# The two halves of the split weights in one buffer, column beside column, in a two-layer hybrid block

## The chip, the cores and the metric

The kernel runs on one core of one Trainium2 chip. The metric is device time in microseconds from launch to end, as the median of repeated runs. The engines are called PE (TensorE; PEld is its weight load), DVE (VectorE), ACT (ScalarE), POOL (GpSimd) and SP (the queue that issues most DMAs).

## The reference

Two layers over 512 tokens of width 1024, in float32. Each layer adds three things to x in turn. First a mixer: one wide projection of the normed x, then three branches (a retention, a gated delta rule with a triangular solve, a dilated attention), each projected back, gated, summed and projected once more. Then an attention to 256 memory tokens. Then a convolved, gated MLP of width 2816.

```python
for l in range(DEPTH):
    x = x + hybrid_mixer(rms_norm(x, norm_mix_g[l]), positions, w_in[l], ...)
    x = x + memory_cross_attention(rms_norm(x, norm_xattn_g[l]), rms_norm(mem, norm_mem_g[l]),
                                   xattn_wq[l], xattn_wkv[l], xattn_wo[l])
    x = x + conv_gated_mlp(rms_norm(x, norm_ffn_g[l]), ffn_w_up[l], ffn_conv_w[l], ffn_conv_b[l],
                           ffn_w_down[l])
return rms_norm(x, final_norm_g)
```

What matters here are the products of x (or of what comes from it) with a weight matrix. They make up nearly all of the arithmetic.

## The kernel before

All weights lie in device memory as slabs of 128 partitions and up to 1024 columns, in the order in which they are used. `slab_load` brings one slab by a DMA of the SP queue into `w`, of which there are two buffers. `slab` cuts it into pieces of `part` columns (512, but for one product) and splits each piece into two parts whose sum is the weight: ACT copies the piece into `wh` in the type fp32r, which rounds it (L203), and DVE subtracts `wh` from `w` and leaves the rest in `wl` (L204). `wh` and `wl` are tiles of their own, 528 columns or 2112 bytes in each partition, with three buffers each. Both instructions are put ahead of other work by `first()`.

The other operand is split in the same way (`xgh`, `xgl` and the like), and `mm3` forms a product of the two sums by three matmuls: high by high (L214), then L215, then L216. The fourth, low by low, is left out. Two kinds of product use it:

- Products with features on the partitions of the result (`fm_tile`, called by `fm_one` and `fm_group`). The weights are the stationary operand, 128 columns to a weight load, and the tokens stream by as the moving operand, 512 at a time (256 for the memory's keys `km`, and for the last tile of the last layer, which is done in two halves). L214 and L215 read `wh`, L216 reads `wl`. A piece of 512 columns has 4 k tiles or column tiles, so 12 matmuls.
- Products with tokens on the partitions (`tm_group`: `rva`, `rvb`, `rg`, `z`, `dv0`, `dv12`, `vm`). Here the tokens are the stationary operand and the weights stream. L214 and L216 read `wh`, L215 reads `wl`. `dv12` takes every 4th token as its stationary columns. `some = 528 // n` says how many k tiles a piece holds. For `rva`, n is 264: two k tiles make a piece of 528 columns, and a slab of three k tiles gives a piece of 528 and one of 264.

The program is laid out by a planner (the Tile framework): it takes the instructions with their priorities, gives each tile a buffer when one of its tag is released, fixes the order on each engine and sets the semaphore waits. A buffer is released when the last instruction that reads or writes its tile is done. Every engine works its own list in order.

The order of stages in a layer: norm sums, `rva` (half of the retention's values and the decays), the gated delta rule's keys, queries and values (`g`), its triangular solve on DVE (lines `fs`, `Tg`), its scan over four blocks, between them the retention's products and further projections (`rqk`, `rvb`, `rg`, `z`, `dqk`, `dv0`, `dv12`), the dilated attention (`ds`, `dt`, `do`), into which the gates (`gate`, `y`) are woven, `wo`, the memory attention (`km`, `xq`, `vm`, `xo`), and the MLP (`up`, `ua`, `uu`, `dn`, at the very end `dl`).

Of the kernel before, what the change touches and what calls it, by code (L numbers as in the profile page):

```python
# [10 lines left out]
F32R = mybir.dt.float32r  # L11
# [21 lines left out]
# The reference's inverse frequencies, which depend on no input.  # L33
# [16 lines left out]
# columns of the constants  # L50
# [6 lines left out]
# columns of the parameters  # L57
# [4 lines left out]
# column ranges of w_in  # L62
# [39 lines left out]
def tile_hybrid(ctx, tc, xT, memT, pos, wts, cst, kst, prm, rows, outT):  # L102
# [53 lines left out]
    def over(ap, n):  # L156
        """[p, a] as [p, a, n], each element n times."""
        a = ap.shape[1]
        return ap.rearrange("p (a o) -> p a o", o=1).to_broadcast([ap.shape[0], a, n])

    def again(ap, n):
        """[p, f] as [p, n, f], n times."""
        return ap.rearrange("p (o f) -> p o f", o=1).to_broadcast([ap.shape[0], n, ap.shape[1]])

# [26 lines left out]
    def slab(n, part=512):  # L191
        """The next slab; part(o, m) gives the two parts of its columns o to o + m."""
        pieces = []
        with first():
            if not loaded:
                slab_load()
            l, s, size, w = loaded.pop(0)
            assert size == n, (l, s, size, n)
            for o in range(0, n, part):
                m = min(part, n - o)  # L200
                wh = wp.tile([P, 528], F32R, tag="wh", name=f"wh{l}_{s}_{o}", bufs=3)
                wl = wp.tile([P, 528], F32R, tag="wl", name=f"wl{l}_{s}_{o}", bufs=3)
                S.activation(wh[:, :m], w[:, o:o + m], AF.Copy)  # L203
                V.tensor_tensor(wl[:, :m], w[:, o:o + m], wh[:, :m], ALU.subtract)  # L204
                pieces.append((wh, wl))

        def cols(o, m):
            h, lo = pieces[o // part]
            assert o % part + m <= part
            return h[:, o % part:o % part + m], lo[:, o % part:o % part + m]  # L210
        return cols
# [6 lines left out]
    def fm_tile(out, w, off, mv, kts, start=True, stop=True, tok=slice(None)):  # L218
        """out[cols, tokens] += W[kts, cols]^T mv[kts]; the weights of the kts stand from off on."""
        for i, kt in enumerate(kts):  # L220
            mm3(out, *w(off + i * P, P), mv[0][:, kt, tok], mv[1][:, kt, tok],
                start and i == 0, stop and i == len(kts) - 1)
# [6 lines left out]
    def fm_group(names, mv, nk):  # L229
        """Four output tiles, a pair of k tiles after the other."""  # L230
        outs = [pd(n) for n in names]
        for k0 in range(0, nk, 2):
            kts = list(range(k0, min(k0 + 2, nk)))
            w = slab(len(kts) * P * len(outs))
            for m, o in enumerate(outs):
                fm_tile(o, w, m * len(kts) * P, mv, kts, k0 == 0, kts[-1] == nk - 1)
        return outs

    def tm_group(name, st, n, kper, tok=blk, nt=NB, pools=(pd,) * NB):
        """out[tokens, cols] for each block of tokens."""  # L240
        outs = [pools[b](f"{name}{b}", (n,)) for b in range(nt)]
        for k0 in range(0, KT, kper):
            kts = list(range(k0, min(k0 + kper, KT)))
            some = 528 // n
            w = slab(len(kts) * n, some * n)
            for i0 in range(0, len(kts), some):
                for b in range(nt):
                    for i in range(i0, min(i0 + some, len(kts))):
                        kt = kts[i]
                        mm3(outs[b], st[0][:, kt, tok(b)], st[1][:, kt, tok(b)], *w(i * n, n),  # L250
                            kt == 0, kt == KT - 1)
        return outs

    def rsqrt(y, v):
        """y = v ** -0.5 by Newton's steps from an estimate by the bits."""
        n = v.shape[1]
        t = small("nt", 32, 2)[:, :n]
        yi = y.bitcast(I32)
        V.tensor_scalar(yi, v.bitcast(I32), 1, None, ALU.arith_shift_right)
        V.tensor_scalar(yi, yi, -1, 0x5F3759DF, ALU.mult, ALU.add)  # L260
        for _ in range(3):
            V.tensor_tensor(t, y, y, ALU.mult)
            V.scalar_tensor_tensor(t, t, -0.5, v, ALU.mult, ALU.mult)
            V.scalar_tensor_tensor(y, t, 1.5, y, ALU.add, ALU.mult)

# [1 line left out]
    def feed(xt, gcol, oh, ol):  # L267
        """x * g in two f32r parts."""
        S.activation(oh, xt, AF.Identity, scale=gcol)
        V.scalar_tensor_tensor(ol, xt, gcol, oh, ALU.mult, ALU.subtract)  # L270
# [9 lines left out]
    def rms(acc, nb, name, perm=False, row=None):  # L280
        """1 / rms as columns [token of the block, block] (then of the blocks of every 4th token) and as rows."""
        rc = small("rc", 8, 3)

        def column(o, tok):
            sp = pg(f"{name}_ss{o}", (nb,))
            for b in range(nb):
                PE.matmul(sp[:, b:b + 1], lhsT=acc[:, tok(b)], rhs=one, start=True, stop=True)
            v = small("rv", 4)[:, :nb]
            V.tensor_scalar(v, sp, 1.0 / D, EPS, ALU.mult, ALU.add)
            rsqrt(rc[:, o:o + nb], v)  # L290

        column(0, blk)
        rps = pg(name + "_rp", (nb * P,))
        for b in range(nb):
            PE.matmul(rps[:, blk(b)], lhsT=rc[:, b:b + 1].to_broadcast([P, P]), rhs=ident,
                      start=True, stop=True)
        rr = tmp("row", [T], name + "_row", 1) if row is None else row
        S.activation(rr, rps, AF.Copy)
        if perm:
            column(nb, lambda b: slice(b, None, NB))  # L300
        return rc, rr
# [52 lines left out]
    def load_tab(j, k0, k1, rr):  # L354
        """The two tables with 1 / rms in them, and the constants of a branch."""
# [7 lines left out]
    def gated(dst, p, rc, half, b, grow):  # L363
        """dst = (1 + tanh(z / 2)) * z / rms' * g, with z = p * rms', for one block of tokens."""
# [6 lines left out]
    def conv_gdn(dst, p, rr, w, name):  # L371
        """dst = 2 silu(conv(p * rr))."""
# [17 lines left out]
    def gdn_decays(l, ab, rb):  # L390
        """Decays and rates: minus the running log decays gp (by tokens of each block), their exponentials,
        and exp(-|gp_i - gp_j|) below the diagonal (in A) and from it on (in attn)."""
# [46 lines left out]
    def norms_of(pool, j, h, src, ssv):  # L439
        """Sums of squares of one head's vectors."""  # L440
# [6 lines left out]
    def gdn_inverse(l, kT, ssv, beta, eg, A):  # L447
        """U = ((I + A)^-1)^T, with A the decayed products of the keys below the diagonal, in A's place."""
# [14 lines left out]
        # diagonal blocks of 32 by substitution, one on each of 64 partitions  # L463
# [27 lines left out]
        # from 32 to 64  # L491
# [18 lines left out]
        # from 64 to 128  # L510
# [24 lines left out]
    def gdn_scan(l, kT, qT, vb, U, attn, ceg, eg, egl, ekl):  # L535
        """The states over the blocks; returns the raw outputs and their sums of squares."""
# [58 lines left out]
    def retention(l, rqk, rv, dec):  # L595
        """Scores within blocks of 128 tokens; what stands before a block comes as a state."""
# [44 lines left out]
    def head_out(o, ssq, gz, rc, scale, oh, ol, pst, name):  # L641
        """The heads' norms, the gates, and the outputs with features on the partitions, in two parts."""
# [24 lines left out]
    def dilated(l, dq, dk, dv0, dv12, kc):  # L667
        """Group 0 over blocks of 128 tokens, groups 1 and 2 over every 4th token; one softmax over all."""
# [5 lines left out]
        for i, o in enumerate((oA, oB)):  # L674
            v8 = st[i].rearrange("p (n e) -> p n e", e=8)
            for n in range(NB):
                for hh in range(2):
# [3 lines left out]
                    # heads hh and hh + 2 stand on the same rows of the array  # L681
# [41 lines left out]
        # the share of each set in the sum over both  # L723
# [37 lines left out]
    def branch(l, j, o, nk, per, rr, merged, last=None):  # L761
        """merged += (1 + tanh(gate / 2)) * (o @ w)."""
# [127 lines left out]
    def update(x, m, p, scale, then):  # L890
        """x += scale * p for one tile of features, and what is next for it."""
# [10 lines left out]
    def cross(l, mm, mrc, mrow, rr, oh, ol):  # L902
        """Attention to the memory: K with features, V with memory tokens on the partitions."""
# [3 lines left out]
        def parts(h, lo, p, row, name):  # L907
            """p * row in two parts."""
# [56 lines left out]
    def final(x, p, t, n):  # L965
        """What follows the last feature tile, for n tokens from t on."""
# [104 lines left out]
    for l in range(L):  # L1071
# [7 lines left out]
        # the memory's norm  # L1079
# [46 lines left out]
def feature_tiles(w, cols):  # L1126
    """[tile, 128, k tiles * 128]: for each tile of 128 columns, its k tiles side by side."""
# [4 lines left out]
def feature_group(w, cols, per=2):  # L1132
    """Slabs of `per` k tiles for all columns: [128, column tile, k tile, 128]."""
# [5 lines left out]
def token_group(w, cols, per):  # L1139
    """Slabs of `per` k tiles: [128, k tile, columns]."""  # L1140
# [9 lines left out]
def slabs_of(i, l):  # L1150
# [4 lines left out]
    # partners of a rotation 16 apart, within 32 partitions  # L1155
# [45 lines left out]
def columns(a):  # L1201
    """[..., k * 128] as [128, ... * k]."""
# [74 lines left out]
```

## Time and profile before

| what | value |
|---|---|
| time, median of 3 runs | 2179.11 us (2178.05 to 2179.14) |
| span of the profiled execution | 2177.5 us |
| PE busy | 2138.7 us, 10665 matmuls |
| PEld busy | 1776.8 us |
| DVE busy | 1369.2 us |
| ACT busy | 927.7 us |
| split of the weights, ACT L203 | 683 instructions, 429.0 us |
| split of the weights, DVE L204 | 683 instructions, 499.7 us |
| granted TensorE clock, mean | 0.991 of full speed |

The profile is one execution of the program. Busy time is the time in which an engine works on an instruction of the program. Matmuls are pipelined: the next starts before the one before it has ended, so the length of one matmul's row (about 0.39 us at 512 columns) is not its share of the time. The distance from one start to the next is. Idle time stands with the instruction before which the engine was idle, and with what released it.

### The profile page before, as it was taken

Reading aid. Unit: us, or ns where it says so; the run is one execution under the profiler, and the core shown is the slowest. Engines: PE = TensorE matmul, PEld = TensorE weight load, DVE = VectorE, ACT = ScalarE, POOL = GpSimd, SP = SyncE. Lnnn points to the kernel's source line nnn. Section 1 sums busy time; section 2 is a strip of 40 time slices with the busy share of each in tenths; the row PEclk is TensorE's granted clock in tenths of the full one; section 3 lists DMA queues with packets and bytes.
Section 4 is the critical chain, followed back from the end, with each engine's and each line's share of the span. In section 5 each row is a group of like instructions: output and inputs, shape, how many; then the busy total and the mean of one; then the engine's idle time right before and its main releaser. Section 6 shows DMA issues by size and latency. Waiting matters only on the chain.

```text
span 2177.5 us, 28783 instructions
## 1 busy us (share of the span) xinstructions
PE 2138.7 (98%) x10665; PEld 1776.8 (82%) x10665; DVE 1369.2 (63%) x2565; ACT 927.7 (43%) x1879; POOL 392.3 (18%) x403
## 2 busy tenths in 40 slices
PE   7899999999999999999999999999999999999997
PEld 7678888888888888888888888978888888888886
DVE  7994585435577775377488846643455787745654
ACT  5734234434355444244356242443344564433433
POOL 6721120001130211011122122100111211100112
PEclk9999999989999999999999999999999999999999
DMA  4324232222333232332323422322223323232332
GB/s 143 90 95 104 77 101 79 59 92 86 99 97 97 88 97 92 102 95 91 112 100 88 115 79 69 92 78 75 75 95 97 107 88 97 90 99 92 97 91 83
DMA packets 69756, 201.58 MB, mean 93 GB/s; under 512 B 18352, under 2 KB 21168, under 8 KB 69104
## 3 DMA queue, kind: packets, MB, share of 16 engines
q1 hardware_dynamic: 67120, 192.34, 28.7%
q0 software_dynamic: 2352, 7.37, 1.2%
q8 instruction: 83, 1.36, 0.3%
q14 instruction: 57, 0.47, 0.1%
q10 hardware_dynamic: 144, 0.04, 0.0%
HBM read 192.85 MB, written 6.88 MB: 92 GB/s over the span
## 4 chain that ended last, share of the span: by engine, by line
PE 87%; DVE 8%; DMA 1%; ACT 1%; issue 1%; SPq 0%; DVEq 0%; ACTq 0%
PE gate L214 4%; PE gate L215 4%; PE gate L216 4%; PE ua L216 3%; PE uu L216 3%; PE uu L214 3%; PE ua L214 3%; PE uu L215 3%; PE ua L215 3%; PE dn L216 3%; PE dn L215 3%; PE dn L214 3%; PE dqk L214 2%; PE dqk L216 2%; PE dqk L215 2%; DVE wl L204 2%
## 5 line engine op out<-in xcount | busy, mean ns | idle before, releaser
L203 ACT ACTIVATE wh<-w 128x512 fp32r<-128x512 f32 (+2 forms) x683 | 429.0, 629 | 868.6 <-PE dn L215 136.6
L204 DVE TENSOR_TENSOR wl<-w,wh 128x512 fp32r<-128x512 f32 (+2 forms) x683 | 499.7, 733 | 386.8 <-ACT wh L203 363.0
L214 PE MATMUL gate<-xgh,wh 128*128 128x512 f32 x384 | 157.6, 410 | 0.0
L215 PE MATMUL gate<-xgl,wh 128*128 128x512 f32 x384 | 156.1, 406 | 0.0
L216 PE MATMUL gate<-xgh,wl 128*128 128x512 f32 x384 | 156.0, 406 | 0.0
L216 PE MATMUL ua<-xgh,wl 128*128 128x512 f32 x320 | 126.2, 394 | 0.0
L216 PE MATMUL uu<-xgh,wl 128*128 128x512 f32 x320 | 126.2, 394 | 0.0
L214 PE MATMUL uu<-xgh,wh 128*128 128x512 f32 x320 | 126.0, 394 | 0.0
L214 PE MATMUL ua<-xgh,wh 128*128 128x512 f32 x320 | 126.0, 394 | 0.0
L215 PE MATMUL ua<-xgl,wh 128*128 128x512 f32 x320 | 125.8, 393 | 0.0
L215 PE MATMUL uu<-xgl,wh 128*128 128x512 f32 x320 | 125.7, 393 | 0.0
L214 PE MATMUL dn<-ah,wh 128*128 128x512 f32 x308 | 121.2, 394 | 0.0
L215 PE MATMUL dn<-al,wh 128*128 128x512 f32 x308 | 121.1, 393 | 0.0
L216 PE MATMUL dn<-ah,wl 128*128 128x512 f32 x308 | 117.7, 394 | 0.0
L1017 POOL TENSOR_TENSOR fya<-fya,fyu 128x512 f32<-128x512 f32 x44 | 72.9, 1657 | 228.7 <-DVE fyu L1001 223.3
L278 POOL TENSOR_TENSOR acc<-acc,sq 128x512 f32<-128x512 f32 x41 | 59.3, 1445 | 250.2 <-ACT sq L277 249.2
L778 POOL TENSOR_TENSOR mg<-mg,g 128x512 f32<-128x512 f32 x32 | 45.9, 1435 | 301.1 <-DVE g L776 301.1
L214 PEld LDWEIGHTS gate<-xgh,wh 128*128 128x128 f32 x384 | 75.0, 195 | 18.5 <-issue 2.6
L216 PEld LDWEIGHTS gate<-xgh,wl 128*128 128x128 f32 x384 | 74.6, 194 | 17.5 <-issue 0.7
L215 PEld LDWEIGHTS gate<-xgl,wh 128*128 128x128 f32 x384 | 74.9, 195 | 16.6 <-issue 0.4
L351 POOL TENSOR_TENSOR rot<-rot,tab 128x512 f32<-128x512 f32 x32 | 47.7, 1501 | 170.4 <-DVE rot L350 160.6
L216 PE MATMUL g<-xgh,wl 128*128 128x512 f32 x192 | 76.8, 400 | 1.6 <-DVE wl L204 1.6
(497 smaller groups left out, 5267.4 us busy)
## 6 DMA issues: line engine op xcount, KB each, us to landing
w<-in_wts SPq DMA_DIRECT2D x331, 512.0 KB, 3.5
tab<-tabs_d POOLq DMA_DIRECT2D x4, 512.0 KB, 4.2
mem<-in_memT POOLq DMA_DIRECT2D x8, 256.0 KB, 3.7
x<-in_xT SPq DMA_DIRECT2D x2, 1024.0 KB, 5.2
x_d<-x SPq DMA_DIRECT2D x8, 256.0 KB, 4.0
x<-x_d SPq DMA_DIRECT2D x2, 1024.0 KB, 5.6
out<-x SPq DMA_DIRECT2D x8, 256.0 KB, 2.3
w<-in_wts SPq DMA_DIRECT2D x7, 256.0 KB, 2.6
```

The costliest lines, as they stand in the source:

```text
L203: S.activation(wh[:, :m], w[:, o:o + m], AF.Copy)
L204: V.tensor_tensor(wl[:, :m], w[:, o:o + m], wh[:, :m], ALU.subtract)
L214: PE.matmul(out, lhsT=lh, rhs=rh, start=start, stop=False)
L215: PE.matmul(out, lhsT=lh, rhs=rl, start=False, stop=False)
L216: PE.matmul(out, lhsT=ll, rhs=rh, start=False, stop=stop)
L278: eng.tensor_tensor(acc, acc, sq, ALU.add)
L351: G.tensor_tensor(t, t, tab[:, 1, :], ALU.mult)
L778: G.tensor_tensor(mt, mt, g, ALU.add)
L1017: G.tensor_tensor(ya, ya, yu, ALU.mult)
```

## The change

The two tiles `wh` and `wl` become one tile `wt` of 1040 floats (4160 bytes) in each partition, of which 1024 are used, with three buffers. `slab` has a new argument `turns`. With `turns`, which all products with features on the partitions use, `wh` is every second float of `wt` from the first on and `wl` every second from the second on: the high and the low part of a column stand side by side, and the columns of either part are 8 bytes apart. Without it (`tm_group`), `wh` is the first half of the 1024 floats and `wl` the second half, each contiguous as before.

With 1024 floats a piece holds at most 512 columns, so `some` becomes `512 // n`. For `rva` that is 1 where it was 2: its pieces have 264 columns, and its slabs of 792, 792 and 528 columns give 3, 3 and 2 pieces. For n of 256 and 512 nothing changes. The instructions that split, load and multiply are the same otherwise, and so are the DMAs. All comments of the file were taken out or left as empty lines, which changes line numbers by a few and no instruction.

```diff
-    def slab(n, part=512):
+    def slab(n, part=512, turns=True):
...
             for o in range(0, n, part):
                 m = min(part, n - o)
-                wh = wp.tile([P, 528], F32R, tag="wh", name=f"wh{l}_{s}_{o}", bufs=3)
-                wl = wp.tile([P, 528], F32R, tag="wl", name=f"wl{l}_{s}_{o}", bufs=3)
+                wt = wp.tile([P, 1040], F32R, tag="wt", name=f"wt{l}_{s}_{o}", bufs=3)[:, :1024]
+                if turns:
+                    wh, wl = (wt.rearrange("p (c s) -> p s c", s=2)[:, i] for i in range(2))
+                else:
+                    wh, wl = (wt.rearrange("p (s c) -> p s c", s=2)[:, i] for i in range(2))
                 S.activation(wh[:, :m], w[:, o:o + m], AF.Copy)
                 V.tensor_tensor(wl[:, :m], w[:, o:o + m], wh[:, :m], ALU.subtract)
                 pieces.append((wh, wl))
...
     def tm_group(name, st, n, kper, tok=blk, nt=NB, pools=(pd,) * NB):
...
-            some = 528 // n
-            w = slab(len(kts) * n, some * n)
+            some = 512 // n
+            w = slab(len(kts) * n, some * n, False)
```

## Rows read from the trace of the kernel before

**Rows 1.** The page, busy time of engines and shares of the chain.
```profile
PE 2138.7 (98%) x10665; PEld 1776.8 (82%) x10665; DVE 1369.2 (63%) x2565; ACT 927.7 (43%) x1879; POOL 392.3 (18%) x403
...
PE 87%; DVE 8%; DMA 1%; ACT 1%; issue 1%; SPq 0%; DVEq 0%; ACTq 0%
```

**Rows 2.** Timeline (start us, length us, engine, line, tiles), feed-forward, matmuls and weight loads.
```profile
1000.19 0.39 PE L214 MATMUL uu<-xgh,wh 128*128 128x512 f32 x1
1000.19 0.19 PEld L215 LDWEIGHTS uu<-xgl,wh 128*128 128x128 f32 x1
1000.42 0.39 PE L215 MATMUL uu<-xgl,wh 128*128 128x512 f32 x1
...
1011.99 0.39 PE L214 MATMUL ua<-xgh,wh 128*128 128x512 f32 x1
```

**Rows 3.** Stretches (from:to, length, busy us (count) by engine); three lines of L204 alone.
```profile
20.00:180.00 160.00, 146.83 (x757) 120.13 (x757) 145.72 (x316) 79.40 (x182) 82.22 (x71) 1.00 0.33 96
760.00:1100.00 340.00, 340.00 (x1488) 276.72 (x1487) 206.64 (x307) 137.97 (x220) 47.03 (x68) 1.00 0.32 100
1100.00:1240.00 140.00, 139.41 (x761) 119.40 (x760) 124.85 (x314) 68.85 (x169) 26.28 (x31) 1.00 0.29 91
...
20.00:180.00 160.00, 36.72 (x45) 1.00 0.33 96
760.00:1100.00 340.00, 86.46 (x122) 1.00 0.32 100
1100.00:1240.00 140.00, 32.52 (x44) 1.00 0.29 91
```

**Rows 4.** Waits (who waited for whom: us in total, times, longest us).
```profile
PE rva L214 <- ACT wh L203: 9.4, 1, 9.4
PE rva L215 <- DVE wl L204: 1.7, 2, 1.4
PE rqk L216 <- DVE wl L204: 0.7, 1, 0.7
...
ACT wh L203 <- PE dn L215: 136.6, 73, 3.1
DVE wl L204 <- ACT wh L203: 363.0, 214, 6.6
```

**Rows 5.** Timeline of `dv12`, whose stationary operand takes every 4th token.
```profile
341.53 0.40 PE L214 MATMUL dv<-wh,xgh 128*128 128x512 f32 x1
...
343.42 0.40 PE L216 MATMUL dv<-wh,xgl 128*128 128x512 f32 x1
```

**Rows 6.** Weight loads (busy us, mean ns | idle before), whole span; `dv12` in 337 to 347.
```profile
L215 PEld LDWEIGHTS uu<-xgl,wh 128*128 128x128 f32 x320 | 60.2, 188 | 14.2
...
L216 PEld LDWEIGHTS dv<-wh,xgl 128*128 128x128 f32 x15 | 4.7, 310 | 0.0
```

**Rows 7.** DVE and ACT instructions by shape (busy us, mean ns | idle before, releaser).
```profile
L204 DVE TENSOR_TENSOR wl<-w,wh 128x512 fp32r<-128x512 f32 x669 | 490.7, 735 | 379.7 <-ACT wh L203 355.9 <-PE dn L215 12.5 <-PE wo L216 6.5
L911 DVE TENSOR_TENSOR qf<-xq,nx_row 128x512 f32<-128x512 f32 x8 | 5.5, 691 | 9.1 <-PE xq L216 8.8
L756 DVE TENSOR_TENSOR dsA<-dsA,dB 128x512 f32<-128x512 f32 x4 | 4.4, 1105 | 2.3 <-PE dB L388 2.3
L911 DVE TENSOR_TENSOR kf<-km,macc 128x256 f32<-128x256 f32 x8 | 3.3, 418 | 0.3
...
L203 ACT ACTIVATE wh<-w 128x512 fp32r<-128x512 f32 x669 | 421.5, 631 | 859.5 <-PE dn L215 132.1 <-PE uu L215 120.4 <-PE gate L215 99.5
L203 ACT ACTIVATE wh<-w 128x264 fp32r<-128x264 f32 x4 | 1.7, 413 | 2.1 <-PE dn L215 2.1
```

**Rows 8.** Timeline of the memory's keys, matmuls of 256 columns.
```profile
641.97 0.28 PE L214 MATMUL km<-mgh,wh 128*128 128x256 f32 x1
...
644.91 0.28 PE L214 MATMUL km<-mgh,wh 128*128 128x256 f32 x1
```

## The prediction

> **What bounds the kernel now.** I read the page first: TensorE is busy for 98% of the span and stands for 87% of the chain that ended last, VectorE (DVE) for 8%, ScalarE (ACT) for 1% [rows 1]. A busy share says nothing of pace, so next the timeline in the feed-forward: the matmuls of 512 columns start every 0.23 us, and the weight load of the next one begins with the matmul before it and is over 0.19 us later, so it lies beside the running matmul [rows 2]. Then the table by stretches, for places where TensorE is not the limit. In 20 to 180 us DVE is busy 145.7 of 160 us and in 1100 to 1240 us 124.9 of 140, while a feed-forward stretch of 340 us has 206.6 us of DVE and 138.0 of ACT [rows 3]. Last the waits: TensorE waited for a split weight piece 9.4 us once at the start, and 6.1 us more in 8 waits, five groups of which the longest and the shortest are shown [rows 4]. So three things can move the time: the pace of the matmuls, the pace of DVE in the two DVE-bound stretches, and what a later piece does there.
>
> **The change part by part.** Instructions and their order in the program stay, except for the first token product of each layer; what changes is where the halves lie. For products with features on the partitions, ACT writes every second float, DVE reads that and writes the floats between, and TensorE loads its stationary columns 8 bytes apart instead of 4. No operand of the kernel before steps by 8 bytes. Rows with 16-byte steps give the far bound, contiguous rows the near one.
>
> *Weight load.* In the last value product (dv12) the stationary operand takes every 4th token, 16 bytes apart. Its load takes 310 ns against 188 ns contiguous [rows 6], and the matmuls of 512 columns start 0.236 us apart (8 steps from 341.53 to 343.42 us, first and last shown) against 0.231 (51 steps from 1000.19 to 1011.99 us) [rows 2, 5, 6]. So at 16 bytes the load itself sets the pace, only 5 ns over today's. There are 669 pieces of 512 columns [rows 7]; 40 in each layer belong to token products, and the other 589 have 12 matmuls each, which with the last tile's own sizes makes 6,879 matmuls of 512 columns and 258 of 256 (the memory's keys and the last tile's halves). The far bound is 6,879 x 5 ns = 34 us, plus 258 x (236 - 118) = 30 us, since those of 256 start every 0.118 us (25 steps from 641.97 to 644.91 us, first and last shown) [rows 8]. The near bound is 0. A gain is excluded: the same 128 columns are loaded as often.
>
> Which end? Three streams give nearly one price for each 16 bytes touched. The moving operand, contiguous, takes 231 ns for 512 floats, which are 128 such units: 1.80 ns. The dv12 load, one unit for each of 128 columns: 236 / 128 = 1.84. On DVE, L756 reads and writes with 16-byte steps: 1105 ns [rows 7]; with a fixed part of 145 ns (691 ns for 512 and 418 for 256 elements, so 1.07 ns for an element) that is 1.88 ns for each. If a unit of 16 bytes costs about 1.85 ns and the engine's own element rate hides what it can, then at 8 bytes two columns share a unit and a load needs 64 x 1.84 = 118 ns: far below 231, and level with the 118 ns of the 256-column matmuls. I take 0 for TensorE. The cover is the running matmul; it is gone when the load alone needs over 231 ns, that is near the 16-byte case.
>
> The Trainium skill ("TensorE: Matmul & The Clock Gate", LDWEIGHTS) lets the load's time depend on the number of columns alone. The 310 against 188 ns above disagree with that for 16-byte steps. By that page this term would be 0 as well.
>
> *DVE's subtraction.* At 16-byte steps 1105 against 691 ns is +414 ns. By the unit price a strided element costs 0.92 ns at 8 bytes, under DVE's own 1.07: +0. In proportion to the units touched (a half per element, between a quarter and one) it would be a third, +140 ns. In the two DVE-bound stretches stand 45 + 44 = 89 subtractions [rows 3]; all of them on the path gives 37 us at the far end, 12.5 us by proportion. I take 0, since the contiguous row shows no price for its own quarter unit beyond DVE's element rate. Elsewhere DVE has room: 122 subtractions x 0.42 = 51 us on 206.6 of 340 us [rows 3].
>
> *ACT's copy.* No ACT row writes with steps; the far bound is DVE's +414 ns. ACT's own rate is (631 - 413) / 248 = 0.88 ns for an element [rows 7], so half a unit, 0.92 ns, for each gives 512 x 0.04 = +20 ns. ACT has the room, and its 1% of the chain hides it: 0.
>
> The Trainium skill ("SBUF — State Buffer", SBUF "cachelines") says two things at once of 16-byte lines: a crossing to a new line pays a penalty, and two hits on a line absorb it. Two floats at 8-byte steps are just two hits. By the second half the sum is what I take; by the first it would be the third that stands in the rival below. The 16-byte rows agree with both, and no row here tells them apart.
>
> *One buffer for both halves.* ACT's next piece now waits until the last matmul that reads the low half (L216) is done, where it waited for the last on the high half (L215): one matmul, 0.23 us, later. ACT waits so often: 73 times for the matmuls of the down products alone, and DVE stood 214 times behind a copy [rows 4]. Queued behind the waiting copy are ACT's evacuations and squares, behind DVE's subtraction the evacuations of PSUM. Two further pieces of 12 matmuls, 24 x 0.231 = 5.5 us, cover copy and subtraction (0.63 + 0.74). So it costs only where TensorE already waits on a piece: 8 waits x 0.23 us = 1.8 us at most; I take 1.
>
> *Pieces of 264 columns.* The first token product splits slabs of 792, 792 and 528 columns into 2 + 2 + 1 pieces now and 3 + 3 + 2 then: 3 more copies and subtractions in each layer. The fixed part of one is 145 ns on DVE and 413 - 264 x 0.88 = 181 ns on ACT: 0.33 x 6 = 2.0 us in series; DVE is nearly full soon after, so I take 1.5. The DMAs, and the queues of SP and POOL, keep what they issue. The first matmul may start 0.2 us earlier, since its copy is of half the width.
>
> **Sum.** The profiled span is 2177.5 us, and about 1.6 us lie around it (the median of the runs is 2179.1). 2179.1 + 0 + 0 + 0 + 1 + 1.5 = 2181.6 us.
>
> **The rivals.**
> *A price in proportion to the units touched* (slower). Load 188 + 122 / 3 = 229 ns, still hidden behind 231; a 256-column matmul goes from 118 to 155 ns, since pace stands 74 ns under the load's length in the 16-byte row: 258 x 37 ns = 9.5 us. DVE 12.5 us. About 2179.1 + 22 + 2.5 = 2204, decided by whether the subtraction's mean rises over some 50 ns. Against it: the equal unit prices. The full 16-byte price on all streams gives 34 + 30 + 37 = 101 us, 2280; it needs a second float in the same 16 bytes to be as dear as the first.
> *Small pieces starve TensorE at the layers' starts* (slower). Three buffers of 264 columns hold 3 x 12 matmuls of 0.12 us = 4.4 us where 528 held 8.8, and DVE has subtractions of x in between, in order. Two waits there on the low half make 1.7 us now [rows 4]. If each of the 8 pieces of a layer waits half a microsecond, that is 8 us: 2190. The point is DVE's other work between two subtractions exceeding 4.4 us.
> *The halves are not told apart by what sets the waits.* Then every piece's first matmul waits for the subtraction, 0.74 us later, which shows only at pieces that come just in time: 9 x 0.5, with the rest about 2186.
> *A better order* (faster). All instructions are planned anew around one buffer and smaller pieces. TensorE idles 13 us of 20 to 180 us [rows 3]; if the new order fills half of it, the time is 2179.1 - 6.6 = 2172.5.
>
> **How the numbers follow.** The forecast, 2177 to 2186, has a chance of 0.50; proportion 0.13 and the full price 0.04; starved starts 0.10; halves not told apart 0.05; a better order 0.18. For a range that leaves out 2 in 10 I go down to 2171 and up to 2204. A measurement tells about 0.2%, 4.4 us, from no change. Below 2174.7: most of the better order, 0.17. Above 2183.5: the two prices 0.17, starved starts 0.10, halves not told apart 0.05, and the forecast's upper end 0.08: 0.40. Within: 0.43.
>
> **What the profile of the changed kernel would show.** The pace of 0.231 us unchanged at 512 columns and 0.118 at 256; load rows at 188 to 200 ns; subtractions at a mean near 735 ns; ACT's copy near 650; ACT's copies released by L216 instead of L215; three more pieces in each layer. Wrong if the subtraction's mean is over 800 ns, or the load is over 230 ns, or the pace of the 512-column matmuls moves at all; or if TensorE's idle time in 0 to 180 us changes by more than 5 us, which would be the order's doing.

## The result, and the profile after

The changed kernel takes 2193.82 us (median of 4 runs, 2191.52 to 2196.09) against 2179.12 us: 0.66% slower, a ratio of 1.0066 with a 95% interval of 1.0052 to 1.0080. Its profiled execution has a span of 2189.7 us against 2177.5. The page, as in [rows 1]:

```profile
PE 2146.1 (98%) x10665; PEld 1828.2 (83%) x10665; DVE 1385.9 (63%) x2571; ACT 953.7 (44%) x1887; POOL 395.9 (18%) x403
...
PE 87%; DVE 8%; ACT 2%; DMA 1%; issue 1%; SPq 0%; DVEq 0%; ACTq 0%
```

All engines have a little more work; nothing new bounds the kernel. In the code after, L208 is ACT's copy, L209 DVE's subtraction, and L219, L220, L221 are the three matmuls that were L214, L215, L216. The groups of instructions and the weight loads (busy us, mean ns | idle before, releaser), beside [rows 6, 7]:

```profile
L220 PEld LDWEIGHTS uu<-xgl,wt 128*128 128x128 f32 x320 | 62.4, 195 | 11.9
...
L220 PEld LDWEIGHTS km<-mgl,wt 128*128 128x128 f32 x64 | 12.5, 196 | 0.1
...
L208 ACT ACTIVATE wt<-w 128x512 fp32r<-128x512 f32 x669 | 445.3, 666 | 787.6 <-PE dn L221 128.7 <-PE uu L221 122.4 <-PE gate L221 92.2
...
L209 DVE TENSOR_TENSOR wt<-w,wt 128x512 fp32r<-128x512 f32 x669 | 493.6, 739 | 387.6 <-ACT wt L208 382.8
...
L209 DVE TENSOR_TENSOR wt<-w,wt 128x264 fp32r<-128x264 f32 x16 | 8.3, 546 | 7.5 <-ACT wt L208 7.5
```

A weight load takes 195 ns where it took 188, ACT's copy 666 where it took 631. The subtraction of 512 columns went from 735 to 739 ns. Timeline of the same part of the feed-forward as [rows 2], first and last of 53 steps:

```profile
999.66 0.40 PE L221 MATMUL ua<-xgh,wt 128*128 128x512 f32 x1
...
1011.93 0.40 PE L220 MATMUL ua<-xgl,wt 128*128 128x512 f32 x1
```

That is 231.5 ns a matmul, as before. The matmuls of 256 columns start 0.120 us apart (ten steps, first and last shown) where it was 0.118 [rows 8]:

```profile
645.28 0.28 PE L219 MATMUL km<-mgh,wt 128*128 128x256 f32 x1
...
646.48 0.28 PE L220 MATMUL km<-mgl,wt 128*128 128x256 f32 x1
```

So the columns that stand 8 bytes apart cost next to nothing here. The stretches, as in [rows 3], with two more of 60 to 80 and 320 to 480 us:

```profile
20.00:180.00 160.00, 147.74 (x734) 124.78 (x735) 143.58 (x315) 81.23 (x182) 83.50 (x73) 0.95 0.29 90
60.00:80.00 20.00, 16.32 (x60) 12.05 (x60) 15.49 (x30) 19.15 (x48) 12.25 (x13) 0.83 0.39 131
320.00:480.00 160.00, 160.00 (x787) 138.39 (x786) 74.80 (x148) 67.51 (x164) 4.23 (x6) 0.99 0.27 86
760.00:1100.00 340.00, 340.00 (x1470) 285.88 (x1469) 209.00 (x308) 140.51 (x215) 45.13 (x67) 1.00 0.30 97
1100.00:1240.00 140.00, 135.37 (x751) 118.23 (x750) 126.08 (x300) 72.09 (x177) 29.80 (x33) 1.00 0.30 92
```

The time went where the prediction had looked for it second, at the layers' starts. In 1100 to 1240 us TensorE is busy 135.4 of 140 us, where it was 139.4. In 20 to 180 us it seems busier than before, but its granted clock is 0.95 where it was 1.00 (0.83 in 60 to 80 us): part of that stretch ran at the lower of the clock's two levels, 1.2 instead of 2.4 GHz. There, after a wait of 2.1 us, the matmuls of 512 columns start 0.43 us apart (nine steps, first and last shown), and a matmul that takes longer counts as busy for longer:

```profile
75.64 0.63 PE L219 MATMUL g<-xgh,wt 128*128 128x512 f32 x1
...
79.47 0.61 PE L219 MATMUL g<-xgh,wt 128*128 128x512 f32 x1
```

In the dilated attention (320 to 480 us) it is the other way round, 0.99 against 0.95 in the kernel before:

```profile
320.00:480.00 160.00, 160.00 (x737) 135.11 (x737) 70.04 (x141) 65.12 (x158) 4.07 (x5) 0.95 0.26 80
```

Over the whole span the mean is 0.991 in both profiles, so the clock does not explain the difference between the two. The waits, beside [rows 4]:

```profile
PE rva L219 <- ACT wt L208: 7.9, 1, 7.9
PE rva L220 <- DVE wt L209: 5.1, 5, 2.0
PE g L219 <- ACT wt L208: 3.4, 2, 2.1
...
PE xo L221 <- DVE vm L960: 1.4, 4, 0.4
...
ACT wt L208 <- PE dn L221: 133.2, 71, 3.1
DVE wt L209 <- ACT wt L208: 390.3, 271, 6.6
```

The first token product waited for the subtraction 5 times and 5.1 us, where it was 2 times and 1.7. ACT is released by L221, the matmul on the low half, where it was L215. The wait of `xo` for `vm` was not there before.

### The profile page after: what moved, and what is told of

It is laid out like the page before. It is cut to its first block, busy times and chain, and to the rows that moved or that the text cites. A ratio compares the mean times of both kernels' runs of the same rounds, so it can differ in the third digit from the quotient of the medians.

```text
span 2189.7 us, 28567 instructions
## 1 busy us (share of the span) xinstructions
PE 2146.1 (98%) x10665; PEld 1828.2 (83%) x10665; DVE 1385.9 (63%) x2571; ACT 953.7 (44%) x1887; POOL 395.9 (18%) x403
## 4 chain that ended last, share of the span: by engine, by line
PE 87%; DVE 8%; ACT 2%; DMA 1%; issue 1%; SPq 0%; DVEq 0%; ACTq 0%
PE gate L219 4%; PE gate L221 4%; PE gate L220 4%; PE ua L220 3%; PE uu L221 3%; PE uu L220 3%; PE ua L221 3%; PE ua L219 3%; PE uu L219 3%; PE dn L221 3%; PE dn L220 3%; PE dn L219 3%; PE dqk L219 2%; PE dqk L220 2%; PE dqk L221 2%; DVE wt L209 2%
## 5 line engine op out<-in xcount | busy, mean ns | idle before, releaser
L208 ACT ACTIVATE wt<-w 128x512 fp32r<-128x512 f32 (+2 forms) x689 | 453.7, 660 | 801.4 <-PE dn L221 133.2
L209 DVE TENSOR_TENSOR wt<-w,wt 128x512 fp32r<-128x512 f32 (+2 forms) x689 | 504.1, 734 | 395.1 <-ACT wt L208 390.3
L219 PE MATMUL gate<-xgh,wt 128*128 128x512 f32 x384 | 154.5, 402 | 0.0
L221 PE MATMUL gate<-xgh,wt 128*128 128x512 f32 x384 | 153.6, 400 | 0.0
L220 PE MATMUL gate<-xgl,wt 128*128 128x512 f32 x384 | 153.4, 399 | 0.0
L221 PE MATMUL uu<-xgh,wt 128*128 128x512 f32 x320 | 126.0, 394 | 0.0
L221 PE MATMUL ua<-xgh,wt 128*128 128x512 f32 x320 | 126.0, 394 | 0.0
L220 PE MATMUL uu<-xgl,wt 128*128 128x512 f32 x320 | 126.0, 394 | 0.0
L220 PE MATMUL ua<-xgl,wt 128*128 128x512 f32 x320 | 126.0, 394 | 0.0
L219 PE MATMUL uu<-xgh,wt 128*128 128x512 f32 x320 | 125.9, 394 | 0.0
L219 PE MATMUL ua<-xgh,wt 128*128 128x512 f32 x320 | 125.9, 394 | 0.0
L220 PE MATMUL dn<-al,wt 128*128 128x512 f32 x308 | 121.3, 394 | 0.0
L219 PE MATMUL dn<-ah,wt 128*128 128x512 f32 x308 | 121.2, 394 | 0.0
L221 PE MATMUL dn<-ah,wt 128*128 128x512 f32 x308 | 117.1, 394 | 0.0
L1022 POOL TENSOR_TENSOR fya<-fya,fyu 128x512 f32<-128x512 f32 x44 | 75.0, 1705 | 228.6 <-DVE fyu L1006 226.8
L221 PEld LDWEIGHTS gate<-xgh,wt 128*128 128x128 f32 x384 | 75.7, 197 | 15.7 <-issue 1.8
L219 PEld LDWEIGHTS gate<-xgh,wt 128*128 128x128 f32 x384 | 75.7, 197 | 14.8 <-issue 1.3
L220 PEld LDWEIGHTS gate<-xgl,wt 128*128 128x128 f32 x384 | 75.8, 197 | 14.1 <-issue 0.7
L219 PE MATMUL g<-xgh,wt 128*128 128x512 f32 x192 | 78.0, 406 | 3.4 <-ACT wt L208 3.4
L221 PE MATMUL g<-xgh,wt 128*128 128x512 f32 x192 | 78.4, 409 | 0.8 <-DVE wt L209 0.7
```

Of the source, the lines that this page charges most:

```text
L219: PE.matmul(out, lhsT=lh, rhs=rh, start=start, stop=False)
L220: PE.matmul(out, lhsT=lh, rhs=rl, start=False, stop=False)
L221: PE.matmul(out, lhsT=ll, rhs=rh, start=False, stop=stop)
L1022: G.tensor_tensor(ya, ya, yu, ALU.mult)
```

## Experiments: the parts of the change, one by one

Theory A: the small pieces of the first token product cost it. Rivals: the single buffer, and the columns 8 bytes apart. Four kernels undo or make one part each.

**One buffer and 8-byte columns, large pieces.** The changed kernel, with pieces of 528 columns.

```diff
-wt = wp.tile([P, 1040], ..., bufs=3)[:, :1024]
+wt = wp.tile([P, 1056], ..., bufs=3)[:, :1056]
...
-            some = 512 // n
+            some = 528 // n
```

> The change with one part undone: the first token product of each layer keeps pieces of 528 columns (one buffer of 1056 floats, high and low still side by side for the other products). Theory A, small pieces of 264 starve the matmuls at the start of each layer (3.1 us lost there in layer 0, 5.7 in layer 1, by the two profiles): 2193.8 - 9 = about 2184, and the first token product ends 3 and 6 us earlier in its layer. Theory B, the 8-byte steps cost it (copy +35 ns, weight load +7 ns): stays at 2191 to 2194. Theory C, one buffer that is released later costs it: stays at 2191 to 2194.

Measured: 2197.62 us, ratio 1.0087 (1.0073 to 1.0100). No theory's time came: A had 2184, B and C 2191 to 2194. Large pieces do not make the changed kernel faster, so the small pieces are not the only cause. That it is even slower is taken up below.

**Small pieces alone.** The kernel before with `some = 512 // n`.

```diff
-            some = 528 // n
+            some = 512 // n
```

> The kernel before with nothing but pieces of 264 columns in the first token product; two tiles, contiguous halves. Theory A: slower than before by about 9 us, 2188, lost in that product. Theories B and C: within 2 us of before, 2179 to 2181.

Measured: 2189.75 us, 1.0053 (1.0039 to 1.0067). That is near theory A's 2188 and outside B's and C's 2179 to 2181: at the pace of the kernel before (231.4 ns between the starts of 512-column matmuls in the feed-forward, in both) small pieces alone cost 10.6 us. In the built program the planner has also put TensorE's instructions in another order, so this is the price of both.

**One buffer and small pieces, halves contiguous.** The changed kernel without the 8-byte steps.

```diff
-    def slab(n, part=512, turns=True):
+    def slab(n, part=512, turns=False):
```

> The change without its 8-byte steps: one buffer, small pieces, but the halves stand one behind the other for all products. Theory A: stays within 2 us of the changed kernel, 2191 to 2194; copy back at 631 ns, weight load at 188 ns, pace of the 256-column keys back from 0.120 to 0.118 us. Theory B: falls back to about 2181. Theory C: 2191 to 2194 as well.

Measured: 2191.56 us, 1.0062 (1.0047 to 1.0076), as theories A and C had it and not B (about 2181). On all five engines its instructions stand in the order of the changed kernel, so the two differ by the steps alone: 2.3 us, and the intervals overlap.

**One buffer alone.** The first of these four, with contiguous halves.

```diff
-    def slab(n, part=512, turns=True):
+    def slab(n, part=512, turns=False):
...
-wt = wp.tile([P, 1040], ..., bufs=3)[:, :1024]
+wt = wp.tile([P, 1056], ..., bufs=3)[:, :1056]
...
-            some = 512 // n
+            some = 528 // n
```

> One buffer alone: contiguous halves of 528 columns in one tile of 1056 floats, large pieces in the first token product. Theory A and theory B: within 3 us of before, 2179 to 2182, with the copies released by the last matmul on the low half. Theory C, the later release costs it: 2188 or more.

Measured: 2183.63 us, 1.0024 (1.0016 to 1.0033), between A's and B's 2179 to 2182 and C's 2188 or more. Against the run with contiguous halves and small pieces this is 7.9 us less, and the intervals don't meet: small pieces cost something also with one buffer (under 2 us of the 7.9 is pace, 231.3 against 231.1 ns a matmul, see below). The stretch in which they do, 1100 to 1120 us, with one buffer alone and then with small pieces added (columns as in [rows 3]):

```profile
1100.00:1120.00 20.00, 19.88 (x135) 18.62 (x134) 15.18 (x41) 8.64 (x19) 5.44 (x4) 1.00 0.39 133
```

```profile
1100.00:1120.00 20.00, 17.54 (x121) 16.39 (x120) 15.30 (x45) 8.62 (x20) 4.33 (x3) 1.00 0.41 125
```

TensorE stands still 2.3 us longer at the start of layer 1.

One thing did not fit. The order of the instructions is the same in this run and in the first one, yet 8-byte columns cost 14.0 us between these two and 2.3 us between the other two. The traces show where: in the first run the 512-column matmuls of the feed-forward start 232.75 ns apart on the mean, in this one 231.1, in the kernels before and after 231.4 and 231.7 (each from some 1,460 distances between starts in 760 to 1100 us). Times 6,879 matmuls, 1.65 ns are 11.4 us.

## Experiments: where the buffers start

What differs besides the steps is the size of a buffer, 4224 or 4160 bytes, and with it the address at which each of the three starts. The distances can be sorted by the buffer whose weights are loaded meanwhile. The start is given as its remainder by 256 bytes; the tokens (`xgh`, `xgl`, and `ah`, `al` for the down products) start at a remainder of 192 in all kernels so far.

| kernel | 192 | 0 | 64 | 128 |
|---|---|---|---|---|
| after, 8-byte columns | 233.0 | 230.8 | 231.5 | |
| large pieces, 8-byte columns | 233.3, 233.2 | | 231.7 | |
| before, contiguous, high half | 230.2 | 232.5 | 233.2 | |
| before, contiguous, low half | 230.8 | 231.1 | | 230.4 |

For the kernel before these means are rough: for one and the same buffer they differ by up to 2 ns between the two layers. Theory S: the pace depends on where the weights start. Rival O: the paces have another cause. The next three kernels change sizes alone; the order of their instructions is that of the kernel they come from.

**All buffers at 192.** The changed kernel with larger buffers.

```diff
-wt = wp.tile([P, 1040], ..., bufs=3)[:, :1024]
+wt = wp.tile([P, 1088], ..., bufs=3)[:, :1024]
```

> The changed kernel with buffers of 4352 bytes where they were 4160, so that all three start 192 bytes past a multiple of 256; order of the instructions as in the changed kernel. Theory S (the pace of the 512-column matmuls depends on where the weights' buffer starts; with columns 8 bytes apart 233.2 ns a matmul from a start at 192, 231.6 at 64 and 230.8 at 0, as the changed kernel and the one with large pieces show buffer by buffer): pace 233.2 where the changed kernel has 231.8, times 6,879 matmuls +10 us, about 2203. Theory O (the paces differ for another reason, and the start is chance): pace 231.8, about 2194.

Measured: 2205.96 us, 1.0124 (1.0107 to 1.0141).

**All buffers at 0.** As that, and the slab's two buffers 32 bytes larger each.

```diff
-w = wp.tile([P, 1024], F32, tag="w", ...)
+w = wp.tile([P, 1032], F32, tag="w", ...)
```

> The changed kernel with buffers of 4352 bytes and the two buffers of the slab 32 bytes larger, so that all three buffers of the halves start at a multiple of 256 bytes; order of the instructions as in the changed kernel. Theory S: pace 230.8 instead of 231.8 ns, about -7 us, 2187. Theory O: pace 231.8, about 2194.

Measured: 2186.06 us, 1.0037 (1.0024 to 1.0050). The timelines of the two, first and last of 52 and of 53 steps:

```profile
999.67 0.39 PE L220 MATMUL uu<-xgl,wt 128*128 128x512 f32 x1
...
1011.80 0.39 PE L221 MATMUL uu<-xgh,wt 128*128 128x512 f32 x1
```

```profile
999.76 0.39 PE L221 MATMUL ua<-xgh,wt 128*128 128x512 f32 x1
...
1011.95 0.39 PE L220 MATMUL uu<-xgl,wt 128*128 128x512 f32 x1
```

233.3 and 230.0 ns a matmul. The same instructions in the same order, at other addresses, differ by 19.9 us; S had 2203 and 2187, O 2194 for both. Theory S holds, O falls.

**Large pieces, all buffers at 0.** The first of these experiments with the same two sizes.

```diff
-wt = wp.tile([P, 1056], ..., bufs=3)[:, :1056]
+wt = wp.tile([P, 1088], ..., bufs=3)[:, :1056]
...
-w = wp.tile([P, 1024], F32, tag="w", ...)
+w = wp.tile([P, 1032], F32, tag="w", ...)
```

> The changed kernel with pieces of 528 columns for the first token product (one buffer, columns 8 bytes apart), and all three buffers at a multiple of 256 bytes where the same kernel with buffers of 4224 bytes had them at 192, 64 and 192; order of the instructions as there. Theory S: pace 230.8 instead of 232.7 ns, -13 us, about 2185. Theory O: pace 232.7, about 2197.6 as there. If small pieces are a cause of their own, this stays below the changed kernel with buffers at 0 by 3 us or more.

Measured: 2181.97 us, 1.0013 (1.0004 to 1.0022), at 230.0 ns, 15.7 us less than with the buffers at 192, 64 and 192. Against the run before this one it prices the small pieces at an equal pace: 4.1 us, and the intervals don't meet.

**Everything moved.** The run with all at 192, with a tile of 64 bytes ahead of the tokens: weights and tokens both start at a remainder of 0.

```diff
+    pad = pp.tile([P, 16], F32, name="pad")
     xgh = pp.tile([P, KT, T], F32R, name="xgh")
```

> The changed kernel with all three buffers of the halves at the same place, as in the run with all at 192, but with everything in the memory 64 bytes further: the halves start at 0 past a multiple of 256, and the tokens (the moving operand) at 0 too, where they started at 192. Order of the instructions as in the changed kernel. If the pace follows the distance between the start of the weights and the start of the moving operand (0 here as in the run at 192): pace 233.4, about 2206. If it follows where the weights start by itself (0 as in the run with all at 0): pace 230.1, about 2186.

Measured: 2206.65 us, 1.0135 (1.0119 to 1.0152), and 233.3 ns, as with both at 192 and not as with the weights alone at 0. The distance between the two operands decides, not the address of one.

**The kernel before, all buffers at 192.** Sizes alone, order as before.

```diff
-wh = wp.tile([P, 528], F32R, tag="wh", ...)
-wl = wp.tile([P, 528], F32R, tag="wl", ...)
+wh = wp.tile([P, 576], F32R, tag="wh", ...)
+wl = wp.tile([P, 576], F32R, tag="wl", ...)
```

> The kernel before, with its two kinds of buffer at 2304 bytes instead of 2112, so that all six start 192 bytes past a multiple of 256; order of the instructions as before. In the kernel before, a matmul of 512 columns whose weights start at 192 took 230.2 (high) and 230.8 ns (low), at 0 and 64 up to 232.5 and 233.2. Theory S (the pace depends on where the weights' buffer starts, for contiguous columns too, and all at 192 is the best of those seen): pace 230.4 where before had 231.6, times 6,879: -8 us, about 2171. Rival: with contiguous columns the mean stays at 231.6, about 2179.

Measured: 2151.87 us, 0.9882 (0.9864 to 0.9901). It is 1.2% faster than the kernel before, and the fastest kernel of this study. Timeline in the feed-forward, first and last of 53 steps:

```profile
899.81 0.39 PE L214 MATMUL dn<-ah,wh 128*128 128x512 f32 x1
...
911.83 0.39 PE L216 MATMUL uu<-xgh,wl 128*128 128x512 f32 x1
```

226.8 ns (226.7 as the mean of all). The direction was expected, the size was not: 230.4 ns and 2171 us were. The paces of the table were taken where buffers of several remainders take turns, and there a buffer at 192 does not show its full pace. 4.7 ns less on 6,879 matmuls would be 32 us; 27 came.

**The kernel before, all buffers at 128.** As that, with `w` of 1048 floats.

```diff
-w = wp.tile([P, 1024], F32, tag="w", ...)
+w = wp.tile([P, 1048], F32, tag="w", ...)
```

> The kernel before with buffers of 2304 bytes, all six 128 bytes past a multiple of 256 (the slab's buffers are 96 bytes larger); order of the instructions as before. In the kernel before, one buffer stood at 128, a low one, with 230.4 ns. Theory S: pace 230.4, about 2171, as at 192. Rival: that one buffer was chance, pace 231.6, about 2179; at 0 and 64 the paces seen reach 233, which would give 2188.

Measured: 2165.18 us, 0.9949 (0.9932 to 0.9967), at 228.9 ns: faster than theory S had it, and its rival's 2179 falls.

**One buffer, both halves at 192.** The run with one buffer alone, with the low half 2304 bytes behind the high one.

```diff
-wt = wp.tile([P, 1056], ..., bufs=3)[:, :1056]
+wt = wp.tile([P, 1152], ..., bufs=3)
...
+wh, wl = wt[:, :576], wt[:, 576:]
```

> One buffer for both halves, contiguous columns, pieces of 528 columns, as in the run with one buffer alone, but the buffer has 4608 bytes with the low half from 2304 on, so that both halves of all three start 192 bytes past a multiple of 256, as in the kernel before at 192; order of the instructions as in the run with one buffer alone. It prices the one buffer at an equal pace, against the kernel before at 192 (2151.9). Pace expected 226.7 to 227 ns by theory S. By the prediction's term (one matmul later, +1 us): 2153. By the idle time that the run with one buffer alone shows on TensorE (5 us more than before): 2157. Rival: both halves in one buffer change the pace by themselves, then it is above 227 by as much as the time is above 2157.

Measured: 2159.72 us, 0.9915 (0.9899 to 0.9931), at 226.7 ns. The pace is the one expected, so the rival falls, and the time is nearer to 2157 than to the 2153 of the prediction's term. Against the kernel before at 192, with the same pace, one buffer costs 7.8 us (the two intervals just touch). Two places can be seen.

The first is the memory attention. DVE's evacuation of its values (`vm`) and TensorE's `xo`, first in the kernel before at 192, then with one buffer (the bracket is idle time and who ended it):

```profile
694.12 0.74 DVE L955 SCALAR_TENSOR_TENSOR vm<-vm,rc,vm 128x512 fp32r<-128x512 f32 x1
...
694.26 0.48 PE L214 MATMUL xo<-pt,vm 128*128 128x512 f32 x1
...
695.40 0.71 PE L216 MATMUL xo<-pt,vm 128*128 128x512 f32 x2
```

```profile
695.25 0.74 DVE L957 SCALAR_TENSOR_TENSOR vm<-vm,rc,vm 128x512 fp32r<-128x512 f32 x1
...
694.56 0.41 PE L945 MATMUL xt<-c,xp 128*128 128x128 f32 x2 [1.27 <-DVE xp L941]
...
696.05 0.50 PE L218 MATMUL xo<-pt,vm 128*128 128x512 f32 x1 [0.40 <-DVE vm L957]
```

With one buffer DVE comes to the evacuation 1.1 us later, 0.9 us of which the kernel had already lost by the last `vm` matmul. Steps of the softmax stand ahead of the evacuation that stood elsewhere, and TensorE waits for `vm`, as nowhere in the kernel before at 192. The waits for `xp` are as long in both, first before at 192, then with one buffer:

```profile
PE xt L943 <- DVE xp L939: 1.6, 3, 0.8
```

```profile
PE xt L945 <- DVE xp L941: 1.6, 2, 1.3
PE xo L218 <- DVE vm L957: 1.3, 4, 0.4
```

That is another order, not a wait for the shared buffer. Between the last `vm` and the last `xo` matmul the kernel with one buffer loses 1.8 us in layer 0 and 1.6 us in layer 1.

The second place costs more. Between the last matmul of `g` and the last of `rqk` in layer 1 the kernel before at 192 needs 24.6 us, the one with one buffer 27.5 us. The two stretches (columns as in [rows 3]):

```profile
1177.70:1202.30 24.60, 24.60 (x122) 20.57 (x122) 24.57 (x55) 7.56 (x12) 5.73 (x6) 1.00 0.26 85
```

```profile
1180.30:1207.80 27.50, 25.80 (x122) 20.14 (x121) 27.47 (x60) 7.22 (x12) 5.09 (x7) 1.00 0.21 67
```

DVE is busy all the time in both, TensorE has as many matmuls, and with one buffer 60 instead of 55 instructions of DVE fall into the stretch, and TensorE stands still for 1.7 us of it. Both programs have the same instructions of DVE, 2,565 in the profile, so here too it is their order. The two built programs differ much: with one buffer more than a fifth of TensorE's instructions and a third to a half of DVE's, by how closely they are compared, stand at another place of their list.

*How firm the two prices are.* The 4.1 us and the 7.8 us are differences of medians, and the granted clock differed: it was 0.988 to 0.991 in the four runs of the kernel before at 192 and 0.991 to 0.994 in the six with one buffer. An estimate takes the clock out by multiplying each run's time with its mean granted clock, since TensorE is busy for 98% of the span. Clocks are recorded to a thousandth, 2 us of a run. It gives 2159 or 2160 us for the kernel before beside every group of these runs and 2173 for the changed one; 2129 for the kernel before at 192 and 2143 with one buffer at 192; 2164 and 2162 for small and large pieces with all buffers at 0; and 2166 for small pieces alone. By that, one buffer costs 13 us, small pieces 2 us with one buffer and 6 to 7 us alone. The spans of the two profiled executions at 192, at mean clocks of 0.991 and 0.992, are 12.1 us apart (2146.3 and 2158.4). So each price is known to a few microseconds only, but one buffer is the larger one either way.

## Experiment: the price of a step

**Columns 16 bytes apart.** Columns c and c + 256 of a piece of 512 share 16 bytes, high and low of each; ACT and DVE work on such a piece in one instruction as before, in two runs of 256 columns.

```diff
-wh, wl = (wt.rearrange("p (c s) -> p s c", s=2)[:, i] for i in range(2))
+wh, wl = (wt.rearrange("p (j b s) -> p s b j", b=2, s=2)[:, i] for i in range(2))
```

> The changed kernel with the columns of either half 16 bytes apart in pieces of 512 columns (columns c and c + 256 stand in the same 16 bytes, high and low of each, so the floats used are the same 1024). Theory U (a price for each 16 bytes touched, about 1.85 ns, hidden under each stream's own rate until it exceeds it): weight load 310 ns, pace 236 ns, subtraction near 1105 ns, ACT's copy near 1130: (236 - 231.8) x 6,600 = 28 us on TensorE, some 30 us for the matmuls of 256 columns, 89 x 0.37 = 33 us of DVE in the two stretches where it is nearly full: about 2285. Theory L (the price of a step rises in proportion to it from 4 bytes on): from 8 to 16 bytes only twice what 4 to 8 bytes cost, so load 209, copy 736, subtraction 747, pace unchanged: about 2196.

Measured: 2303.37 us, 1.0573 (1.0550 to 1.0596). The load, the copy and the subtraction of this kernel (L213, L214), and ten steps of the memory's keys:

```profile
L233 PEld LDWEIGHTS uu<-xgh,wt 128*128 128x128 f32 x320 | 99.1, 310 | 0.0
...
L213 ACT ACTIVATE wt<-w 128x512 fp32r<-128x512 f32 x589 | 668.3, 1142 | 510.5 <-PE dn L233 91.9 <-PE gate L233 72.8 <-PE dqk L233 68.0
L214 DVE TENSOR_TENSOR wt<-w,wt 128x512 fp32r<-128x512 f32 x589 | 689.4, 1173 | 346.5 <-ACT wt L213 343.3 <-ACT egl L445 1.1 <-ACT k L754 1.1
```

```profile
676.21 0.39 PE L231 MATMUL km<-mgh,wt 128*128 128x256 f32 x1
...
678.55 0.40 PE L232 MATMUL km<-mgl,wt 128*128 128x256 f32 x1
```

Theory U is borne out on all streams: load 310 ns (forecast 310), copy 1142 (1130), subtraction 1173 (1105), the pace of 512 columns 237 (236), and that of 256 columns 234 ns, double. From 4 to 8 bytes load, copy, subtraction and the two paces moved by 7, 35, 4, 0 and 2 ns. The time, 2303, is 18 us above that sum. Its two runs had a mean granted clock of 0.986 and 0.982, where the changed kernel had 0.990 and 0.991, and 0.0065 of 2303 us would be 15 us (an estimate).

## Why the prediction was right and wrong, step by step

The range of 2171 to 2204 held the time, and "slower by over 0.2%", at 0.40, is what came. The likeliest case, 2181.6 and no change that can be told, did not. That the range held it is in part luck: its upper end came from the price in proportion to the units touched, and the 0.40 mostly from the two prices for a step, starved starts and halves that are not told apart. Of these only starved starts were seen, in part. The largest term that was measured, the one buffer, stood in the sum at 1 us and in no rival for a slower kernel.

*Weight load, 188 to 200 ns:* 195. *Subtraction near 735:* 739. *ACT's copy near 650:* 666, so half a unit for each float was a little low. It is hidden, as forecast: from the run with one buffer at 192 to the one with 8-byte columns, large pieces and buffers at 0 the time rises by 22.3 us, and the pace alone, 3.3 ns times 6,879, makes 22.7. The price of 1.85 ns for each 16 bytes touched, drawn from three streams of the trace of before, stands, and the run with 16-byte steps shows its steep part. The rivals "in proportion" and "full price" fall with that.

*TensorE 0.* The sum was right within 2 us, the reason was not whole. "The cover is the running matmul" takes the 231 ns for a fixed duration of 512 columns. They are not: with contiguous weights the matmuls start 226.7, 228.9 or 231.4 ns apart, with weights 8 bytes apart 230.0 or 233.3, by where the weights start beside the tokens. The kernel before stood at 231.4 with buffers of mixed remainders, the changed one at 231.7, and only for that reason did the steps cost nothing. With each at the best place seen here, columns 8 bytes apart cost 3.3 ns a matmul, 23 us. The mark "wrong if the pace moves at all" was the right one; in the kernel with large pieces it moved by 1.3 ns.

The Trainium skill ("TensorE: Matmul & The Clock Gate", Step-by-step: what each phase is for) says that TensorE has two independent read ports and that loading the next weights takes no read bandwidth from the running matmul. No run here shows ports. But 230.0 against 233.3 ns, from the same instructions in the same order and by the distance of the two operands alone, says that in this kernel the load and the matmul beside it are not independent in time.

*One buffer, +1 us.* This is the step that failed most: 7.8 us at an equal pace, 13 by the estimate at an equal clock. The wait that was priced is there, L221 releases ACT instead of L215, one matmul later. What was wrong is the sentence ahead of it, that the instructions and their order stay. The rival of a better order says that all is planned anew, and prices that as a chance of a gain only. The order came out worse, in `xo` by 1.8 and 1.6 us and at the start of layer 1 by 2.9. How much of the whole is the later release and how much the order was not separated: one buffer with the old order was not tried.

*Pieces of 264 columns, +1.5 us.* By medians they cost 4.1 us with one buffer and 10.6 alone, with the order of TensorE changed in both cases. The rival "small pieces starve TensorE" named the mechanism: `rva` waits for the subtraction 5 times and 5.1 us instead of twice and 1.7, and 2.3 us are lost at the start of layer 1. It had put that at half a microsecond for each of 8 pieces in each of two layers, 8 us; fewer pieces wait, some of them longer (2.0 us). The first matmul came 1.5 us earlier in the changed kernel's profile (after 7.9 instead of 9.4 us), but it starts at 8.0 to 8.1 us also in three profiles with pieces of 528 columns (the kernel before at 192 and at 128, one buffer alone), so hardly more than the 0.2 us of the prediction belongs to the pieces. The 264-column subtraction itself takes 546 ns on the mean where it took 427; why was not looked into.

*The sum.* By medians one buffer 7.8, small pieces 4.1 and 0.3 ns of pace (2 us) make 14, of a measured 14.7. By the estimate at an equal clock they are 13, 2 and 2, which make 17, of 14 (2173 less 2159). Both are prices from other placements, and small pieces alone at 10.6 us show that the parts do not simply add, since each is planned in its own order. In the forecast the three stood at 1, 1.5 and 0.

*"The halves are not told apart"* (2186) falls: L219 and L220 start on the copy's or the subtraction's release in the waits above, each by its own. The mark on the order, TensorE's idle time in 0 to 180 us changing by more than 5 us, did not show either (22.6 us before, 21.6 after, at the lower clock): the idle time that the change added stands at the start of layer 1, 4 us in 1100 to 1240 us.

## What to carry to other kernels

Look at where operands that are read together start before judging a change of their layout: buffer sizes moved this kernel by 1.2% with no instruction changed, and the best place found was contiguous weights at the same remainder by 256 bytes as the moving operand. Where a planner orders the work, price a change of tiles as a change of order too, which can lose as well as gain, and compare with a kernel whose order is the same. Price a strided operand by the 16-byte units it touches against the stream's own rate: here it was nearly hidden at two floats a unit (up to 3.3 ns a matmul at the best places) and not at one. Where prices are a few microseconds, look at the granted clock of each run before comparing medians.

## What was not expected of the hardware

- The 512-column matmuls start 226.7 ns apart with contiguous weights at the tokens' remainder, 228.9 with the weights 64 bytes behind it (128 against 192), and 231.4 with mixed places. With 8-byte columns it is the reverse: 233.3 at the same remainder (also with both moved by 64 bytes), 230.0 with the weights 64 bytes past it. What in the memory makes this was not found.
- A buffer's pace seems to depend on the others that take turns with it: a high half at 192 among mixed buffers has 230.2 ns, among buffers all at 192 226.7.
- The granted clock at the start of layer 0 (60 to 80 us) is 1.00 in the kernel before and 0.83 in the changed one. But it is 0.83 also in the kernel before at 192, which has the old order and the large pieces, so the change is not needed for it. The kernel before, then the one at 192:

```profile
60.00:80.00 20.00, 18.07 (x89) 14.40 (x88) 16.52 (x28) 18.68 (x52) 12.49 (x13) 1.00 0.37 118
60.00:80.00 20.00, 17.34 (x70) 13.41 (x69) 16.54 (x28) 18.72 (x50) 12.50 (x13) 0.83 0.35 118
```
